# A decoder trunk in fp32: the norm between sub-layers with wide sums and a wide root, and the first chunk's products in two sums

## The chip, the core and the metric

One core of one Trainium2 chip. The metric is the time of one execution of the program on the device, in microseconds (us), as the median over runs. TensorE multiplies matrices, VectorE, ScalarE and GpSimd work elementwise, SyncE starts most DMA transfers.

## The reference

Two layers, each with three sub-layers: an FFN (half step), a token mixer with three attention branches, and a second FFN. 256 tokens, 1024 channels, float32. Between one sub-layer and the next stand two RMS norms, one on the output y of the old sub-layer and one on the new residual x:

```python
def rms_norm(x, g):
    xf = x.astype(jnp.float32)
    y = xf * lax.rsqrt(jnp.mean(xf * xf, axis=-1, keepdims=True) + EPS)
...
def swiglu(h, w_gate, w_up, w_down):
    return (jax.nn.silu(h @ w_gate) * (h @ w_up)) @ w_down

def modulate(x, g_pre, shift, scale):
    return rms_norm(x, g_pre) * (1 + scale) + shift

def residual_add(x, y, g_post, gate, res_w):
    return x + res_w * (1 + gate) * rms_norm(y, g_post)
...
        h = modulate(x, norm_pre[l, 0], mod[:, 0, 0], mod[:, 0, 1])
        x = residual_add(x, swiglu(h, ffn_w_gate[l, 0], ffn_w_up[l, 0], ffn_w_down[l, 0]), norm_post[l, 0], mod[:, 0, 2], 0.5)
        h = modulate(x, norm_pre[l, 1], mod[:, 1, 0], mod[:, 1, 1])
```

## The kernel before

Channels lie on the 128 partitions, in KC = 8 chunks; the 256 tokens lie along the free dimension. Every activation and weight is split into a high part in a reduced float32 format (fp32r) and the low rest, and each product is three matmuls, high x high, high x low and low x high (`mm3`, L170). Weights come from HBM through SyncE's queue as raw tiles of 512 KB; `wsplit` (L147) makes the high part on ScalarE (L165) and the low part on VectorE (L166). The vectors of the modulation (`modc`) come from products with `ada_w` on VectorE (L118), between other work. The framework's scheduler orders each engine's instructions by priorities and by `issue_after` pairs; each engine then runs them strictly in that order. PSUM has three banks "lin", four "att" and one "sum".

At the end of a sub-layer `out_tile` (L313) takes the eight chunks of its output: ScalarE squares them, VectorE adds up the squares of chunks 0 to 5 in `sqp`, those of chunks 6 and 7 stay apart (`sqs`); the scaled output goes to `yT`. At the start of the next, `enter` (L249) does the following.

- `mean_of` (L182) sums the squares over the channels with narrow matmuls: the squares are the stationary operand, a column of 1/n the moving one, so 128 tokens lie on the partitions of each of two columns. `rstd_from` (L194) takes the root of the 128x2 result on ScalarE (L200), its reciprocal on VectorE (L201), and spreads it over all partitions by two matmuls with a broadcast and the identity matrix (L204).
- Row k of the unnormalized new input, `acol * x`, is made for each chunk k, where `x` is the old residual plus `yT * rs`. For chunk 0, `ax` and `ay` (L258, L259) are made ahead of the root, so that one multiplication (L271) and one addition (L272) lead to the row.
- Of six weight tiles (`first`) the products of each row are summed, 18 matmuls for one k (L283), each 258 wide: two more columns carry the shift.
- In the midst of it the second norm is summed (`sqx`) with the same two functions; its root `rpre`, copied to SBUF on ScalarE (L291), scales the six results afterwards (`evac`, `evac_first`), and `finish` fills `hT`, the normalized input in high and low parts, for all further products of the sub-layer (`modulated`, L240: a VectorE, a ScalarE and a VectorE instruction for each chunk).

`enter` runs five times: for two mixers and three FFNs. The first FFN starts with `opening` (L789), which computes its norm from the input alone; after the last FFN the output norm is applied and stored (L884 to L889). Inside a mixer `sub_norm` (L441) uses the same functions for two small norms.

Of the kernel before, what the change touches and what calls it, by code (L numbers as in the profile page):

```python
# [28 lines left out]
def trunk(ctx, tc, x, c, vecs, ada_w, w_gate, w_up, w_down, w_in, w_uq, w_ukv, w_branch, w_out, rope, out):  # L29
# [22 lines left out]
    onesn = {}  # L52
    for n in (D, 256, 128):
        onesn[n] = const.tile([128, 1], F32, name=f"ones{n}")
        nc.vector.memset(onesn[n], 1.0 / n)
# [138 lines left out]
    def rstd_from(t, ahead=False):  # L194


        st = t[:, 0:2]
# [10 lines left out]
    def rstd_of(sqs, n, ahead=False):  # L208
        return rstd_from(mean_of(sqs, n, ahead), ahead)
# [15 lines left out]
    gap(res, 64, "gap0")  # L225
# [3 lines left out]
    hact = lambda i, k: hT[i][k]  # L229
    FIRST = 2176  # L230
# [18 lines left out]
    def enter(l, s, first, lent):  # L249

        acol = small.tile([128, KC], F32, name="acol")
        scale_col(l, s, acol)
        ax, ay = small.tile([128, S], F32, name="sq"), sqx
        with tc.high_priority(offset=2000):
            nc.vector.tensor_scalar(ax, xT[0], acol[:, 0:1], None, op0=OP.mult)  # L258
            nc.vector.tensor_scalar(ay, yT[:, 0, :], acol[:, 0:1], None, op0=OP.mult)  # L259
        rs, _ = rstd_of([sqp] + sqs, D, True)  # L260
        bb = modc[:, l, 3 * s, :][:, :, None].to_broadcast([128, KC, 2])
        lent = [t[:, :KC * (S + 2)].rearrange("p (k n) -> p k n", k=KC) for t in lent]
        hi, lo = [t[:, :, S:S + 2] for t in lent]
        nc.vector.tensor_copy(hi, bb)
        nc.vector.tensor_sub(lo, bb, hi.bitcast(F32))
        done = []
        for k in range(KC):
            hi, lo = [t[:, k, :] for t in lent]
            with tc.high_priority(offset=2000):
                if k == 0:  # L270
                    nc.vector.tensor_mul(ay, ay, rs)  # L271
                    head = nc.vector.tensor_add(hi[:, :S], ay, ax)  # L272
                with tc.issue_after(head.ins) if k < 2 else ExitStack():
                    nc.vector.tensor_mul(yT[:, k, :], yT[:, k, :], rs)
                nc.vector.tensor_add(xT[k], xT[k], yT[:, k, :])
                if k > 0:
                    hold[:] = [nc.scalar.activation(hi[:, :S], xT[k], AF.Copy, scale=acol[:, k:k + 1])]
                last = nc.vector.scalar_tensor_tensor(lo[:, :S], xT[k], acol[:, k:k + 1], hi[:, :S].bitcast(F32),
                                               op0=OP.mult, op1=OP.subtract)
                sum_sq(sqx, xT[k], k == 0)  # L280
            order = [(t, i, j) for i, j in ((0, 0), (1, 0), (0, 1)) for t in first]
            for (p, w, cols), i, j in (order if k < KC - 1 else sorted(order, key=lambda o: first.index(o[0]))):
                done.append(nc.tensor.matmul(p, w(i, k, cols), (hi, lo)[j], start=(k == 0 and i == j == 0),  # L283
                                             stop=(k == KC - 1 and j == 1)))
        hold.append(last)
        with tc.high_priority(offset=2000):
            with tc.issue_after(done[16 * len(first)].ins):
                t = mean_of([sqx], D, True)
            bc, _ = rstd_from(t, True)
            rp = small.tile([128, S], F32, name="rpre", bufs=1)  # L290
            nc.scalar.copy(rp, bc)  # L291

        def finish(ks=range(KC)):
            with tc.high_priority(offset=2000):
                for k in ks:
                    modulated(l, s, k, acol, bc)

        return rp, finish
# [14 lines left out]
    def out_tile(n, p, g):  # L313
        if n < KC - 1:
            if n < KC - 2:
                sum_sq(sqp, p, n == 0)
            else:
                sqs[:] = [small.tile([128, S], F32, name="pn", bufs=2) for _ in range(2)]
                nc.scalar.activation(sqs[0], p, AF.Square)
            done = nc.scalar.activation(yT[:, n, :], p, AF.Copy, scale=g[:, n:n + 1])  # L320
            if n == KC - 3:
                late[:] = [done]
        else:
            nc.scalar.activation(sqs[1], p, AF.Square)
            nc.vector.tensor_scalar(yT[:, n, :], p, g[:, n:n + 1], None, op0=OP.mult)
# [4 lines left out]
    def ffn(l, f, s, opening=None, ahead=None):  # L330
        with ExitStack() as es:
# [43 lines left out]
            if opening is None:  # L375
                todo = ([(0, n) for n in range(6)] + [(1, n) for n in range(6)] + todo[12:])
                first = [(ps(S + 2, kind="lin" if i < 3 else "att"),) + weights(*t) for i, t in enumerate(todo[:6])]
                rp, finish = enter(l, s, first, [wdp.tile([128, FIRST], F32R, name=f"wd8_{i}") for i in range(2)])
# [35 lines left out]
    def mixer(l, s):  # L414
        with ExitStack() as es:
# [25 lines left out]
            def sub_norm(src, nk, gcol, name):  # L441
# [3 lines left out]
                t = mean_of([sq], nk * 128, kind="att")  # L445
                yield
                rs, ins = rstd_from(t)
# [189 lines left out]
            first = [(ps(S + 2, kind="lin" if i < 3 else "att"), wb[i // 2], cols[i % 2]) for i in range(6)]  # L637
            gap(mp, 64, "gap2")
            rp, finish = enter(l, s, first, [mp.tile([128, FIRST], F32R, name=n) for n in ("ga", "gb")])
# [149 lines left out]
    def opening(W, evac):  # L789

        with tc.tile_pool(name="open", bufs=2) as op:
            with tc.high_priority(offset=2000):
# [9 lines left out]
                bc, _ = rstd_of([yT[:, 0, :]], D)  # L802
                rp = small.tile([128, S], F32, name="rpre", bufs=1)
                nc.scalar.copy(rp, bc)
# [173 lines left out]
```

## Time and profile before

| | us |
|---|---|
| median of 3 runs | 1303.7 (1302.9 to 1312.09) |
| profiled execution | 1309.85 |
| its span, first to last instruction | 1308.1 |
| TensorE busy (matmul) | 1267.7 (97%) |
| VectorE busy | 983.1 (75%) |
| ScalarE busy | 752.1 (57%) |

Matmuls are pipelined: the record of one is longer (0.28 us) than the distance to the next (0.11 us), so the starts of successive rows tell how fast TensorE goes. The granted clock is TensorE's clock as a share of 2.4 GHz; its two levels are 1.0 and 0.5 (1.2 GHz). A matmul in plain float32 is two records.

### The profile page before, as it was taken

To read this page: it belongs to the slowest core of one execution; us is meant where nothing else is said; L and a number is where in the kernel's file an instruction comes from. 1 tells how busy PE (TensorE), PEld (TensorE's weight loads), DVE (VectorE), ACT (ScalarE), POOL (GpSimd) and SP (SyncE) were. 2 spreads that over 40 slices of the span, in tenths; PEclk is the share of its full clock that TensorE was granted. 3 is DMA by queue.
4 is the path that set the end of the run, shared out by engine and by line. 5 is a ranking of instruction groups with operands and counts; after the bars stand their busy time and mean duration, and the time that the engine had idled before them with its cause. 6 is when DMAs were issued, how large, how long until landed. Compare 5 with 4: busy or idle time off the path is not lost. (4 is left out here: it accounts for less than half of the span.)

```text
span 1308.1 us, 26637 instructions
## 1 busy us (share of the span) xinstructions
PE 1267.7 (97%) x10752; PEld 1233.9 (94%) x10752; DVE 983.1 (75%) x1706; ACT 752.1 (57%) x1287; POOL 70.9 (5%) x140
## 2 busy tenths in 40 slices
PE   7999899999999999999999999999999999999997
PEld 6999899999899999999999999999998999999997
DVE  8987766767779789877679886585777779996553
ACT  4654454666866656445555454467567666655551
POOL 0011000000000000110000110000000000000000
PEclk9999998999999999999999999999999999999999
DMA  9997883545476666988727997626466666396550
GB/s 356 368 316 271 276 275 120 198 135 188 156 262 224 203 216 211 328 303 274 270 99 269 314 316 266 237 75 206 140 208 209 222 236 246 113 321 207 189 192 33
DMA packets 82925, 295.75 MB, mean 226 GB/s; under 512 B 9201, under 2 KB 9585, under 8 KB 82802
## 3 DMA queue, kind: packets, MB, share of 16 engines
q1 hardware_dynamic: 64370, 226.94, 50.0%
q0 software_dynamic: 18432, 67.12, 15.5%
q8 instruction: 84, 1.38, 0.4%
q14 instruction: 39, 0.32, 0.1%
HBM read 292.97 MB, written 1.05 MB: 225 GB/s over the span
## 5 line engine op out<-in xcount | busy, mean ns | idle before, releaser
L166 DVE TENSOR_TENSOR wlo<-raw,whi 128x1024 fp32r<-128x1024 f32 (+3 forms) x382 | 450.3, 1197 | 117.4 <-ACT whi L165 112.7
L171 PE MATMUL lin<-h,whi 128*128 128x256 f32 x1808 | 501.9, 279 | 4.5 <-DVE m L356 4.3
L173 PE MATMUL lin<-h,wlo 128*128 128x256 f32 x1808 | 499.3, 277 | 0.8 <-DVE wlo L166 0.8
L172 PE MATMUL lin<-h,whi 128*128 128x256 f32 x1808 | 499.3, 277 | 0.2
L165 ACT CAST whi<-raw 128x1024 fp32r<-128x1024 f32 (+3 forms) x382 | 389.4, 1034 | 172.7 <-PE lin L172 105.0
L171 PEld LDWEIGHTS lin<-h,whi 128*128 128x128 f32 x1808 | 337.8, 188 | 8.2 <-DVE m L356 5.3
L173 PEld LDWEIGHTS lin<-h,wlo 128*128 128x128 f32 x1808 | 339.7, 188 | 1.4 <-DVE wlo L166 1.4
L172 PEld LDWEIGHTS lin<-h,whi 128*128 128x128 f32 x1808 | 338.8, 188 | 1.0 <-DVE h L247 1.0
L118 DVE SCALAR_TENSOR_TENSOR ada<-ada,cb 128x1024 f32<-128x1024 f32 x128 | 154.4, 1221 | 49.5 <-DMA ada<-in_ada_w_dram 49.5
L171 PE MATMUL lin<-mid,whi 128*128 128x256 f32 x592 | 163.5, 276 | 1.1 <-DVE m L356 1.1
L172 PE MATMUL lin<-mid,whi 128*128 128x256 f32 x592 | 163.4, 276 | 0.0
L173 PE MATMUL lin<-mid,wlo 128*128 128x256 f32 x592 | 163.4, 276 | 0.0
L132 POOL DMA_DIRECT2D ada<-in_ada_w_dram x128 | 68.1, 532 | 1047.5 <-DVE ada L118 1016.3
L171 PEld LDWEIGHTS lin<-mid,whi 128*128 128x128 f32 x592 | 111.1, 188 | 1.3 <-DVE m L356 1.3
L172 PEld LDWEIGHTS lin<-mid,whi 128*128 128x128 f32 x592 | 111.1, 188 | 0.0
L173 PEld LDWEIGHTS lin<-mid,wlo 128*128 128x128 f32 x592 | 111.1, 188 | 0.0
L360 ACT CAST mid<-m 128x256 fp32r<-128x256 f32 x88 | 34.9, 409 | 115.8 <-DVE m L356 115.5
L171 PE MATMUL lin<-ybhi,whi 128*128 128x256 f32 x192 | 54.0, 281 | 2.0 <-DVE gb L514 2.0
L172 PE MATMUL lin<-yblo,whi 128*128 128x256 f32 x192 | 53.3, 278 | 0.0
L173 PE MATMUL lin<-ybhi,wlo 128*128 128x256 f32 x192 | 53.3, 278 | 0.0
L361 DVE TENSOR_TENSOR mid<-m,mid 128x256 fp32r<-128x256 f32 x88 | 36.3, 422 | 20.6 <-ACT mid L360 20.6
L171 PEld LDWEIGHTS lin<-ybhi,whi 128*128 128x128 f32 x192 | 36.1, 188 | 2.4 <-DVE gb L514 2.4
(272 smaller groups left out, 1957.4 us busy)
## 6 DMA issues: line engine op xcount, KB each, us to landing
ada<-in_ada_w_dram POOLq DMA_DIRECT2D x128, 512.0 KB, 5.7
raw<-in_mix_w_in_dram SPq DMA_DIRECT2D x100, 512.0 KB, 5.2
raw<-in_ffn_w_gate_dram SPq DMA_DIRECT2D x88, 512.0 KB, 5.8
raw<-in_ffn_w_up_dram SPq DMA_DIRECT2D x88, 512.0 KB, 6.0
raw<-in_ffn_w_down_dram SPq DMA_DIRECT2D x80, 512.0 KB, 5.1
raw<-in_mix_w_branch_dram SPq DMA_DIRECT2D x24, 512.0 KB, 6.9
oada<-in_ada_w_dram SPq DMA_DIRECT2D x16, 512.0 KB, 7.6
raw<-in_mix_w_out_dram SPq DMA_DIRECT2D x16, 512.0 KB, 5.0
```

The source lines that it names most:

```text
L118: return nc.vector.scalar_tensor_tensor(raw, raw, 1.0, cb, op0=OP.mult, op1=OP.mult, accum_out=modc[:, l, i, k:k + 1])
L132: nc.gpsimd.dma_start(raw, ada_w[al, i * D + k * 128:i * D + k * 128 + 128, :])
L165: nc.scalar.copy(hi, raw)
L166: nc.vector.tensor_sub(lo, raw, hi.bitcast(F32))
L171: nc.tensor.matmul(o, whi, ahi, start=start, stop=False)
L172: nc.tensor.matmul(o, whi, alo, start=False, stop=False)
L173: nc.tensor.matmul(o, wlo, ahi, start=False, stop=stop)
L360: nc.scalar.copy(mid[0][n], m)
L361: anchor[:] = [nc.vector.tensor_sub(mid[1][n], m, mid[0][n].bitcast(F32))]
```

## The change

- `mean_of` sums with a stationary 128x128 matrix of -1 (`negones`), the squares moving: one 128x256 float32 matmul for each tile of squares, and the sum stands on all partitions. `rstd_from` takes the root of the 128x256 result (scale -1/n) and the reciprocal 256 wide; the matmuls that spread it and the copies to SBUF go.
- `out_tile` adds the squares of chunk 6 to `sqp` too; chunk 7 alone stays apart.
- `enter` makes row 0 twice: once of the residual alone (`xrow`, with the shift's columns), once of the update alone (`yT * rs * acol`, 256 wide). Both are multiplied with the six weight tiles and summed in the same bank: 36 matmuls for chunk 0 in place of 18. The residual's first six products stand ahead of the last matmul of the sum of squares, its other twelve behind it. `xrow` lies in the last chunks of `hT`, or in the FFN's weight buffers behind a mixer. The residual's chunk 0 is updated behind chunk 1's.
- Four of the six first results lie in "att" banks and two in "lin" banks (three and three before).

```diff
-    def mean_of(sqs, n, ahead=False, kind="sum"):
-        t = ps(512, kind=kind)
-        st = t[:, 0:2]
+    def mean_of(sqs, ahead=False, kind="sum", behind=None):
+        t = ps(kind=kind)
         for i, sq in enumerate(sqs):
-            with tc.high_priority(offset=2000 if ahead and i == len(sqs) - 1 else 0):
-                for h in range(2):
-                    nc.tensor.matmul(st[:, h:h + 1], sq[:, h * 128:(h + 1) * 128], onesn[n],
-                                     start=(i == 0 and h == 0), stop=(i == len(sqs) - 1), skip_group_check=True)
+            with ExitStack() as es:
+                if behind is not None and i == len(sqs) - 1:
+                    es.enter_context(tc.issue_after(behind()))
+                es.enter_context(tc.high_priority(offset=2000 if ahead else 0))
+                nc.tensor.matmul(t, negones, sq, start=i == 0, stop=i == len(sqs) - 1, skip_group_check=True)
         return t
...
-            rs = small.tile([128, 2], F32, name="rs")
-            ins = nc.scalar.activation(rs, st, AF.Sqrt, bias=epst)
+            rs = small.tile([128, S], F32, name=name, bufs=1)
+            ins = nc.scalar.activation(rs, t, AF.Sqrt, bias=epst, scale=-1.0 / n)
             nc.vector.reciprocal(rs, rs)
-            bc = t[:, 256:512]
-            for h in range(2):
-                nc.tensor.matmul(bc[:, h * 128:(h + 1) * 128], rs[:, h:h + 1].to_broadcast([128, 128]), ident,
-                                 start=True, stop=True, skip_group_check=True)
-        return bc, ins
+        return rs, ins
...
+            nc.scalar.activation(xrow[0][:, :S], xT[0], AF.Copy, scale=acol[:, 0:1])
+            nc.vector.scalar_tensor_tensor(xrow[1][:, :S], xT[0], acol[:, 0:1], xrow[0][:, :S].bitcast(F32),
+                                           op0=OP.mult, op1=OP.subtract)
+            nc.vector.tensor_scalar(ay, yT[:, 0, :], acol[:, 0:1], None, op0=OP.mult)
...
+        def x_part():
+            products(xrow, slice(0, S + 2), 0, start=True, which=((0, 0),))
+            return done[-1].ins
+
+        rs, _ = rstd_from(mean_of([sqp] + sqs, True, behind=x_part), D, True)
+        products(xrow, slice(0, S + 2), 0, which=((1, 0), (0, 1)))
...
                 if k == 0:
-                    nc.vector.tensor_mul(ay, ay, rs)
-                    head = nc.vector.tensor_add(hi[:, :S], ay, ax)
-                with tc.issue_after(head.ins) if k < 2 else ExitStack():
+                    head = nc.vector.tensor_mul(hi, ay, rs)
+                with tc.issue_after(head.ins):
                     nc.vector.tensor_mul(yT[:, k, :], yT[:, k, :], rs)
...
+            products(row, slice(0, S + 2 if k else S), k, stop=k == KC - 1)
         hold.append(last)
         with tc.high_priority(offset=2000):
-            with tc.issue_after(done[16 * len(first)].ins):
-                t = mean_of([sqx], D, True)
-            bc, _ = rstd_from(t, True)
-            rp = small.tile([128, S], F32, name="rpre", bufs=1)
-            nc.scalar.copy(rp, bc)
+            t = mean_of([sqx], True, behind=lambda: done[19 * len(first)].ins)
+            rp, _ = rstd_from(t, D, True, "rpre")
...
         if n < KC - 1:
-            if n < KC - 2:
-                sum_sq(sqp, p, n == 0)
-            else:
-                sqs[:] = [small.tile([128, S], F32, name="pn", bufs=2) for _ in range(2)]
-                nc.scalar.activation(sqs[0], p, AF.Square)
+            sum_sq(sqp, p, n == 0)
```

How the rows of the engines move. In the names, `mid` is the FFN's inner activation, `wd_0` and `wd_1` its weights, `pn` the squares of the last chunk, `ga` and `gb` the rows of `enter` in the first mixer, `h_132` and `h_133` (in `hT`) the residual's row. TensorE before, end of the first FFN and start of the first mixer:

```order
L171 MATMUL lin<-mid_21_171,wd_0_2538 128x256
L172 MATMUL lin<-mid_21_193,wd_0_2538 128x256
L173 MATMUL lin<-mid_21_171,wd_1_2539 128x256
L190 MATMUL sum<-ones_86,sqp 128x1 x2
L190 MATMUL sum<-ones_86,pn 128x1 x4
L204 MATMUL sum<-ident,rs 128x128 x2
L283 MATMUL lin<-ga,whi 128x258 x3
L283 MATMUL att<-ga,whi 128x258 x3
L283 MATMUL lin<-ga,wlo 128x258 x3
```

TensorE of the change, the end of the same last output tile:

```order
L167 MATMUL lin<-mid_18_162,wd_0_2527 128x256
L168 MATMUL lin<-mid_18_184,wd_0_2527 128x256
L187 MATMUL sum<-sqp,negones 128x256
L169 MATMUL lin<-mid_18_162,wd_1_2528 128x256
L167 MATMUL lin<-mid_19_163,wd_0_2527 128x256
```

and some rows on, up to the first products:

```order
L167 MATMUL lin<-mid_21_165,wd_0_2527 128x256
L168 MATMUL lin<-mid_21_187,wd_0_2527 128x256
L169 MATMUL lin<-mid_21_165,wd_1_2528 128x256
L263 MATMUL lin<-h_132,whi 128x258 x2
L263 MATMUL att<-h_132,whi 128x258 x4
L187 MATMUL sum<-pn,negones 128x256
L263 MATMUL lin<-h_132,wlo 128x258 x2
L263 MATMUL att<-h_132,wlo 128x258 x4
L263 MATMUL lin<-h_133,whi 128x258 x2
L263 MATMUL att<-h_133,whi 128x258 x4
L263 MATMUL lin<-ga,whi 128x256 x2
L263 MATMUL att<-ga,whi 128x256 x4
```

The sum of `sqp` has moved into the last tile's products, the residual's products stand around the last sum, and the broadcast (L204) is gone.

VectorE before, end of the first mixer and start of the second FFN; here `wd_0` and `wd_1` hold the rows of `enter`, `wlo` is a low part of weights:

```order
L217 TENSOR_TENSOR sqp<-sqp,sq 128x256
L166 TENSOR_TENSOR wlo<-raw,whi 128x1024 x4
L325 TENSOR_SCALAR yT<-lin,gcol 128x256
L201 RECIPROCAL rs<-rs 128x2
L264 CAST wd_0_6031<-modc 128x8x2
L265 TENSOR_TENSOR wd_1_6032<-modc,wd_0_6031 128x8x2
L271 TENSOR_TENSOR sqx<-sqx,sum 128x256
L272 TENSOR_TENSOR wd_0_6031<-sqx,sq 128x256
```

VectorE of the change, the same place:

```order
L207 TENSOR_TENSOR sqp<-sqp,sq 128x256
L162 TENSOR_TENSOR wlo<-raw,whi 128x1024 x2
L207 TENSOR_TENSOR sqp<-sqp,sq 128x256
L162 TENSOR_TENSOR wlo<-raw,whi 128x1024 x2
L252 CAST wd_0_6026<-modc 128x2
L252 CAST wd_0_6024<-modc 128x7x2
L255 SCALAR_TENSOR_TENSOR wd_1_6027<-xT,acol,wd_0_6026 128x256
L253 TENSOR_TENSOR wd_1_6027<-modc,wd_0_6026 128x2
L253 TENSOR_TENSOR wd_1_6025<-modc,wd_0_6024 128x7x2
L330 TENSOR_SCALAR yT<-lin,gcol 128x256
L195 RECIPROCAL rpost<-rpost 128x256
L277 TENSOR_TENSOR wd_0_6024<-sqx,rpost 128x256
```

The addition of the seventh square now stands between the four splits of weights, and the shift's columns and the residual's low part have come ahead of L330 (L325 before) and of the reciprocal.

## Rows read from the trace of the kernel before

**Rows 1.** The page: granted TensorE clock, tenths of full speed, 40 slices of 32.7 us

```profile
PEclk9999998999999999999999999999999999999999
```

**Rows 2.** Waits: engine, line, what it waited for; us in total, times, longest

```profile
PE sum L204 <- DVE rs L201: 4.3, 7, 0.7
...
PE lin L171 <- ACT rot L708: 3.6, 2, 1.8
```

**Rows 3.** Timeline of TensorE, an FFN's end: start, length (us), [idle before, for whom]

```profile
206.53 0.50 PE L190 MATMUL sum<-ones,sqp 128*128 128x1 f32 x4
...
208.47 0.71 PE L204 MATMUL sum<-ident,rs 128*128 128x128 f32 x4 [0.55 <-DVE rs L201]
210.25 0.98 PE L283 MATMUL lin<-ga,whi 128*128 128x258 f32 x3 [1.06 <-DVE ga L272]
```

**Rows 4.** Timeline, the same end: ScalarE, then VectorE

```profile
204.69 0.39 ACT L319 ACTIVATE pn<-lin 128x256 f32<-128x256 f32 x1 [2.28 <-PE lin L173]
...
206.73 0.38 ACT L324 ACTIVATE pn<-lin 128x256 f32<-128x256 f32 x1 [1.29 <-PE lin L173]
...
209.68 0.42 DVE L272 TENSOR_TENSOR ga<-sqx,sq 128x256 fp32r<-128x256 f32 x1
```

**Rows 5.** Timeline, a mixer's end: TensorE, then VectorE

```profile
1109.28 0.50 PE L190 MATMUL sum<-ones,sqp 128*128 128x1 f32 x4
...
1113.13 0.60 PE L283 MATMUL lin<-wd,whi 128*128 128x258 f32 x3 [1.06 <-DVE wd L272]
...
1106.22 4.62 DVE L166 TENSOR_TENSOR wlo<-raw,whi 128x1024 fp32r<-128x1024 f32 x4
1110.76 0.48 DVE L325 TENSOR_SCALAR yT<-lin,gcol 128x256 f32<-128x256 f32 x1
```

**Rows 6.** Stretches behind two starts: us, busy PE, PEld, DVE, ACT, POOL, PEclk, DMA, GB/s

```profile
210.30:217.00 6.70, 6.70 (x34) 6.70 (x35) 6.70 (x20) 3.55 (x9) 0.00 (x0) 0.55 0.01 2
...
474.90:479.50 4.60, 4.60 (x26) 4.60 (x27) 4.60 (x14) 1.97 (x5) 0.00 (x0) 0.63 0.66 252
```

**Rows 7.** Stretches behind the two waits for L708

```profile
346.00:349.50 3.50, 3.50 (x19) 3.50 (x18) 3.42 (x6) 2.91 (x8) 0.00 (x0) 0.51 0.20 81
...
985.00:988.50 3.50, 2.98 (x24) 2.59 (x23) 3.42 (x6) 3.36 (x11) 0.00 (x0) 1.00 0.21 87
```

**Rows 8.** Lines L201, L551, L302: VectorE rows, ns min/median/max

```profile
L201 DVE RECIPROCAL rs<-rs x16: 153/166/166, 10.8 to 1299.0; 128x2 f32<-128x2 f32 x16
...
L551 DVE RECIPROCAL r<-sm x32: 145/160/167, 315.4 to 1054.3; 128x2 f32<-128x2 f32 x32
...
L302 DVE TENSOR_SCALAR shift<-lin x15: 148/149/152, 230.3 to 1132.5; 128x1 f32<-128x1 f32 x15
```

**Rows 9.** Timeline of TensorE: an fp32 matmul 256 wide, in two records

```profile
268.33 0.28 PE L173 MATMUL lin<-h,wlo 128*128 128x256 f32 x1
268.44 0.59 PE L589 MATMUL att<-P,negtri 128*128 128x256 f32 x2
268.88 0.38 PE L590 MATMUL att<-P,negones 128*128 128x128 f32 x2
```

**Rows 10.** Timeline of TensorE: the second norm amid the first products

```profile
1126.32 0.50 PE L190 MATMUL sum<-ones,sqx 128*128 128x1 f32 x4
1126.68 0.49 PE L283 MATMUL lin<-wd,wlo 128*128 128x258 f32 x2
...
1127.96 0.60 PE L204 MATMUL sum<-ident,rs 128*128 128x128 f32 x4
```

**Rows 11.** Timeline of VectorE: the first rows for hT

```profile
1129.01 0.87 DVE L244 SCALAR_TENSOR_TENSOR pn<-xT,acol,sum 128x256 f32<-128x256 f32 x2 [0.55 <-ACT rpre L291]
```

**Rows 12.** Timeline of VectorE: the first normalized row of the opening

```profile
12.76 0.48 DVE L824 SCALAR_TENSOR_TENSOR pn<-xT,acol,rpre 128x256 f32<-128x256 f32 x1 [0.26 <-ACT rpre L804]
```

**Rows 13.** Timeline, the end: TensorE's sums, VectorE's first output

```profile
1297.28 0.50 PE L190 MATMUL sum<-ones,sqp 128*128 128x1 f32 x4
...
1299.97 0.95 DVE L887 TENSOR_TENSOR yT<-yT,sum 128x768 f32<-128x768 f32 x1 [0.80 <-PE sum L204]
```

More of the change, by code (lines that the diff above doesn't have):

```diff
@@ L51, in trunk @@
     nc.vector.tensor_copy(identb, ident)
[L52 to L55, printed above, removed]
     epst = const.tile([128, 1], F32, name="epst")
@@ L223, in gap @@
         pool.tile([128, nbytes // 4], F32, name=name)
-    gap(res, 64, "gap0")
+    gap(res, 160, "gap0")
     hTt = [res.tile([128, KC, S], F32R, name=f"h{i}") for i in range(2)]
@@ L229, in trunk @@
     hact = lambda i, k: hT[i][k]
+    xrow_h = [t[:, KC - 2:, :].rearrange("p k n -> p (k n)")[:, :S + 2] for t in hTt]
     FIRST = 2176
@@ L247, in modulated, with enter @@
         anchor[:] = [nc.vector.scalar_tensor_tensor(lo, t, b, hi.bitcast(F32), op0=OP.add, op1=OP.subtract)]
-    def enter(l, s, first, lent):
+    def enter(l, s, first, lent, xrow):
         acol = small.tile([128, KC], F32, name="acol")
         scale_col(l, s, acol)
[L256 to L260, printed above, removed]
+        ay = sqx
@@ new lines, in enter, with products @@
+        done = []
+        def products(act, cols_of, k, start=False, stop=False, which=((0, 0), (1, 0), (0, 1))):
+            order = [(t, i, j) for i, j in which for t in first]
+            for (p, w, cols), i, j in (order if not stop else sorted(order, key=lambda o: first.index(o[0]))):
+                done.append(nc.tensor.matmul(p[:, cols_of], w(i, k, cols), act[j][:, cols_of], start=start and i == j == 0,
+                                             stop=stop and j == 1, skip_group_check=True))
@@ L267, in enter @@
+        def x_part():
[3 more added lines that the diff above has]
+        products(xrow, slice(0, S + 2), 0, which=((1, 0), (0, 1)))
         for k in range(KC):
-            hi, lo = [t[:, k, :] for t in lent]
+            row = [t[:, k, :] for t in lent]
+            hi, lo = [t[:, :S] for t in row]
             with tc.high_priority(offset=2000):
                 if k == 0:
-                    nc.vector.tensor_mul(ay, ay, rs)
-                    head = nc.vector.tensor_add(hi[:, :S], ay, ax)
-                with tc.issue_after(head.ins) if k < 2 else ExitStack():
+                    head = nc.vector.tensor_mul(hi, ay, rs)
+                with tc.issue_after(head.ins):
@@ L281, in enter @@
[L281 to L284, printed above, removed]
+                if k == 0:
+                    head = nc.vector.scalar_tensor_tensor(lo, yT[:, 0, :], acol[:, 0:1], hi.bitcast(F32),
+                                                          op0=OP.mult, op1=OP.subtract)
+                else:
+                    add = nc.vector.tensor_add(xT[k], xT[k], yT[:, k, :])
+                    if k == 1:
+                        head = add
+                    hold[:] = [nc.scalar.activation(hi, xT[k], AF.Copy, scale=acol[:, k:k + 1])]
+                    last = nc.vector.scalar_tensor_tensor(lo, xT[k], acol[:, k:k + 1], hi.bitcast(F32),
+                                                          op0=OP.mult, op1=OP.subtract)
+                    if k == 1:
+                        with tc.issue_after(head.ins):
+                            nc.vector.tensor_add(xT[0], xT[0], yT[:, 0, :])
+                        sum_sq(sqx, xT[0], True)
+                    sum_sq(sqx, xT[k], False)
@@ L323, in out_tile @@
         else:
-            nc.scalar.activation(sqs[1], p, AF.Square)
+            sqs[:] = [small.tile([128, S], F32, name="pn", bufs=2)]
+            nc.scalar.activation(sqs[0], p, AF.Square)
             nc.vector.tensor_scalar(yT[:, n, :], p, g[:, n:n + 1], None, op0=OP.mult)
@@ L376, in ffn @@
                 todo = ([(0, n) for n in range(6)] + [(1, n) for n in range(6)] + todo[12:])
-                first = [(ps(S + 2, kind="lin" if i < 3 else "att"),) + weights(*t) for i, t in enumerate(todo[:6])]
-                rp, finish = enter(l, s, first, [wdp.tile([128, FIRST], F32R, name=f"wd8_{i}") for i in range(2)])
+                first = [(ps(S + 2, kind="lin" if i < 2 else "att"),) + weights(*t) for i, t in enumerate(todo[:6])]
+                rp, finish = enter(l, s, first, [wdp.tile([128, FIRST], F32R, name=f"wd8_{i}") for i in range(2)],
+                                   [wdp.tile([128, S + 2], F32R, name=f"wd16_{i}") for i in range(2)] if s == 2 else xrow_h)
                 evac(*todo[0], first[0][0], rp)
@@ L444, in sub_norm @@
                     sum_sq(sq, src[:, k, :], k == 0)
-                t = mean_of([sq], nk * 128, kind="att")
+                t = mean_of([sq], kind="att")
                 yield
-                rs, ins = rstd_from(t)
+                rs, ins = rstd_from(t, nk * 128, name="rpost" if nk > 1 else "rpre")
                 hi = mp.tile([128, nk, S], F32R, name=name + "hi")
@@ L636, in mixer @@
             wb = [win(1536 + 256 * i, 256) for i in range(3)]
-            first = [(ps(S + 2, kind="lin" if i < 3 else "att"), wb[i // 2], cols[i % 2]) for i in range(6)]
+            first = [(ps(S + 2, kind="lin" if i < 2 else "att"), wb[i // 2], cols[i % 2]) for i in range(6)]
             gap(mp, 64, "gap2")
-            rp, finish = enter(l, s, first, [mp.tile([128, FIRST], F32R, name=n) for n in ("ga", "gb")])
+            rp, finish = enter(l, s, first, [mp.tile([128, FIRST], F32R, name=n) for n in ("ga", "gb")], xrow_h)
             qkb = mp.tile([128, 8, S], F32, name="km")
@@ L801, in opening @@
                 nc.vector.tensor_add(yT[:, 0, :], yT[:, 0, :], yT[:, 1, :])
-                bc, _ = rstd_of([yT[:, 0, :]], D)
-                rp = small.tile([128, S], F32, name="rpre", bufs=1)
-                nc.scalar.copy(rp, bc)
+                rp, _ = rstd_of([yT[:, 0, :]], D, name="rpre")
             acol = small.tile([128, KC], F32, name="acol")
```

22 lines of the change are left out of this document (8 added, 14 removed).

## The prediction

> **What bounds the kernel now.** I read the page first, then the waits of TensorE, then the timeline of each engine around one change of sub-layer, then the stretches with their granted clock.
>
> TensorE is busy nearly all the time. What it loses is in few places: the row of the granted clock has its only dips there [rows 1], and the waits of TensorE name them: seven times it waits for the root of the output norm (L201) [rows 2]; five of these stand at the start of a sub-layer. Such starts are the entry of two mixers and of three FFNs (the first FFN has an opening of its own). One of them, at an FFN's end: the last product is issued just before T = 206.53, and the first product of the mixer starts at 210.25, 3.72 us later [rows 3]. In between stands a chain: Square on ScalarE [rows 4], twelve narrow sums, root, reciprocal, broadcast matmuls, a multiplication and an addition on VectorE. At a mixer's end it is 3.85 us, from 1109.28 to 1113.13, and VectorE comes to it with four splits of weights still queued [rows 5].
>
> Behind each such gap the clock is at 1.2 GHz for a while: 0.55 of full speed over 6.70 us once, 0.63 over 4.60 us at the four others (one stands for them) [rows 6]. Lost: 0.45 x 6.70 + 4 x 0.37 x 4.60 = 9.8 us. So the five starts cost 5 x 3.8 us of gap and 9.8 us of clock, some 29 us, 2% of the span.
>
> **The chain of the output norm.** Step by step from T at an FFN's end. The running sum sqp now takes row 6 as well, and its matmul stands in TensorE's row 10 products ahead of the last. Its turn comes at T - 10 x 0.113 = 205.40 (0.11 us a product, L173 to L589 [rows 9]); Square of row 6 ended at 204.69 + 0.39 = 205.08 [rows 4], the addition on VectorE (0.42 us, as any 256-wide one with two operands [rows 4]) at 205.53, so TensorE waits 0.13 us. A 128x256 fp32 matmul takes 0.44 us of the row (L589 to L590) [rows 9]. The last product is thus over at T + 0.6. Square of row 7 then runs to T + 1.2; meanwhile TensorE does the first six x products, 258 wide, so 0.12 each, to T + 1.3, then the last sum, to T + 1.75. The root, 256 wide, takes about what Square takes, 0.42 with its start: T + 2.25. Then the reciprocal, then a multiplication 0.45, and 0.15 until the product starts (L272 ends at 210.10, the product starts at 210.25) [rows 3, 4].
>
> **What the trace does not show: a reciprocal 256 wide.** It shows it 2 wide, with medians of 166 and 160 ns at two lines and 167 ns as the longest; a one-column operation takes 149 ns [rows 8]. If it streams like other VectorE operations, 256 elements take 0.42 us. If what the two elements take above 149 ns is their price, it is 5.5 to 9 ns each, 1.6 to 2.4 us in all. I take 2.0 us, since the rows of the operation itself are the nearest ones, and keep 0.42 and 2.4 as ends.
> The Trainium skill (VectorE: DVE Perf Modes, "First, the fixed hardware budget") says that Reciprocal is an iterative divide with a repeat count of 8. Read as 8 cycles of its 0.96 GHz for each element, an estimate by that page is 2.13 + 0.15 = 2.3 us, and the sum below would be +7 in place of +5 us; no row here shows it.
>
> With 2.0 us the products of the update start at T + 2.25 + 2.0 + 0.45 + 0.15 = T + 4.85, against T + 3.72 before: **+1.1 us at three starts**. The other twelve x products end at T + 1.75 + 12 x 0.12 = T + 3.2 and then TensorE waits 1.7 us. The 18 x products are work added (2.15 us), hidden in the chain either way. The 18 products of the update take the place of the old first row's 18.
> At a mixer's end VectorE sets the time. Its reciprocal stood behind L325, which started at 1110.76 and held the queue some 0.4 us, to 1111.15 [rows 5]. Now an addition and the low x part, 0.4 us each, and two more small copies, 0.2 each, come before it and one multiplication of 0.3 goes: 0.9 us (estimates from the 256-wide rows). So the reciprocal starts at 1112.05, the update at 1112.05 + 2.0 + 0.6 = 1114.65, against 1113.13 [rows 5]: **+1.5 us at two starts**. TensorE also stands in the row for sqp, whose addition is queued behind two of the four splits, 1.15 us each; that lies inside this chain. All five: 3 x 1.1 + 2 x 1.5 = +6.3 us.
>
> **The clock.** A wait of 1.7 us after six and then twelve products is shorter than the gap before. The trace holds two waits of 1.8 us at full speed, both for L708 [rows 2]: behind one, at 345, the clock fell to 0.51, behind the other, at 984, it stayed [rows 7]. So I count half of 9.8 us regained, -4.9 (ends: 0 and -9.8).
>
> **The second norm** (of the new residual, in the midst of the first products): four narrow sums (1126.32 to 1126.68) and four broadcast records (0.60 with their ends, some 0.4 of the row) go; one 0.44 us matmul comes [rows 10]: -0.3 us each, -1.4 in all. Its reciprocal lies off TensorE's path but in VectorE's queue ahead of the rows that fill hT, which the next products read. A ScalarE copy and a broadcast round trip go, 1.8 us of reciprocal comes; I take 0.5 us each, +2.5 (ends 0 and +9.0).
>
> **The rest.** Opening: VectorE waits only 0.26 us for the root's copy [rows 12]; the reciprocal now stands behind both products with ada_w: +1.2 (ends +0.1 and +2). End: the sums started at 1297.28 and the first output at 1299.97, 2.69 us [rows 13]; now 0.6 + 0.44 + 0.46 for sums and root, 2.0 and two issues, 3.56: +0.9. Four inner norms of the mixer, under products of other pieces: +0.5. The high and low x parts are made before the last product ends, under it.
>
> **Sum:** 6.3 - 4.9 - 1.4 + 2.5 + 1.2 + 0.9 + 0.5 = +5.1 us. The profiled execution of before took 1309.85 us (span 1308.1 and 1.75 around it), so 1315.0 for one like it; the median of the runs is 1303.7, 6.15 lower, and on that scale the forecast is 1308.8, +0.4%. Its own range, by the clock's ends and the reciprocal's, is 1301 to 1316.
>
> **Rivals.**
> *The wide reciprocal streams* (0.42 us). For it: the other 256-wide VectorE rows shown take 0.42 and 0.48 us [rows 4, 5]; against it: the 11 to 18 ns above. Then the update starts at T + 3.27 at an FFN's end (-0.45 x 3), at 1113.07 at a mixer's (-0.1 for both), TensorE's x products end at T + 3.2, so it hardly waits and the clock stays: -9.8. Second norm -1.4, end -0.7, opening +0.1: -13.2, **1290.5**.
> *VectorE's queue behind the first products decides.* The first row for hT came at 1129.01 [rows 11]; if the 1.8 us of the second reciprocal reach TensorE whole at all five starts (+9.0 in place of +2.5), and the clock falls at four of five (-2.0 in place of -4.9): 5.1 + 6.5 + 2.9 = +14.5, **1318.2**, slower. It decides once VectorE, between the end of the first products and the last row of hT, has no idle time left; for it speaks that VectorE is busy all through the stretch behind a start [rows 6], against it the 0.55 us in which it idles before that first row [rows 11].
> *A price in between*, 1 us: the start comes 0.5 us later at two places and 0.1 at three, the clock stays: about -6, **1298**.
>
> **How the numbers follow.** Forecast 0.42, streaming 0.38, VectorE's queue 0.15, in between 0.05. One per cent, about what a measurement of this kernel can tell from no change, is 1290.7 and 1316.7. Faster by more: half of the streaming case and a little, 0.22. Slower by more: most of the queue's case and the upper end of the forecast's, 0.16. Within: 0.62. The range takes in the middle of the streaming case with some 2 us below it, and the queue's: 1288 to 1318.
>
> **What would show it.** The row of the reciprocal 256 wide on the changed line: 1.6 us or more makes the forecast or the queue's case, 0.45 or less the streaming one. The start of the first product with ga or wd after the last product of the sub-layer: T + 4.9 or T + 3.3. The row of the granted clock: dips at two or three of five, or at none. The stretch of 7 us behind the first products: fewer matmuls in it than before means that the queue's case is at work. I would be wrong altogether if TensorE stood for the sums' matmul in the middle of the last products for over a microsecond, or if the x products waited for their weights' low parts.

## The result, and the profile after

The changed kernel took 1328.99 us (median of 4 runs, 1327.54 to 1331.92), the kernel before 1307.89 us (4 runs, 1302.9 to 1322.0): 1.014 of it, 95% interval 1.0095 to 1.0186. The forecast was 1308.8 us with a range to 1318: it is slower, and outside the range. The forecast stands on the 1303.7 us of the first three runs; in the rounds of the experiments the kernel before had medians of 1310.7 to 1314.7 us. So part of the distance in microseconds is the base. As a ratio, the top of the range (1.011 of its base) lies inside the interval, and the forecast itself (1.004) below it. The profiled executions took 1328.8 and 1309.85 us, their spans are 1327.1 and 1308.1 us: 19.0 us to be explained.

The page after, granted clock:

```profile
PEclk9999999999999999999999999999999999999999
```

The dip of [rows 1] is gone. That row could show only the longest dip, at the first start; the four shorter ones of [rows 6] do not bring a slice of 32.7 us below 9 tenths. So the stretches behind two starts have to tell (columns as in [rows 6]; 144 products each):

```profile
212.50:230.00 17.50, 17.48 (x144) 17.45 (x145) 17.04 (x38) 10.04 (x20) 0.00 (x0) 1.00 0.15 40
...
477.50:495.00 17.50, 17.50 (x145) 17.37 (x145) 17.03 (x40) 10.21 (x21) 0.00 (x0) 1.00 0.19 63
```

Clock 1.00 where it was 0.55 and 0.63. In the same rows VectorE is busy 17.0 of 17.5 us; that will matter. The reciprocal 256 wide, by its line:

```profile
L195 DVE RECIPROCAL rpre<-rpre x8: 1694/1746/1748, 11.9 to 1141.0; 128x256 f32<-128x256 f32 x8
L195 DVE RECIPROCAL rpost<-rpost x8: 1745/1752/1753, 210.2 to 1317.2; 128x256 f32<-128x256 f32 x8
```

1.75 us, near the 2.0 us that were taken. A start at an FFN's end, timeline of TensorE, ScalarE and VectorE, which answers to [rows 3] and [rows 4]:

```profile
206.60 0.70 PE L187 MATMUL sum<-sqp,negones 128*128 128x256 f32 x2
206.95 0.47 PE L169 MATMUL lin<-mid,wd 128*128 128x256 f32 x1
...
208.28 0.40 PE L263 MATMUL lin<-h,whi 128*128 128x258 f32 x2
...
209.00 0.61 PE L187 MATMUL sum<-pn,negones 128*128 128x256 f32 x2
...
212.52 0.47 PE L263 MATMUL lin<-ga,whi 128*128 128x256 f32 x2 [1.45 <-DVE ga L277]
...
209.66 0.48 ACT L194 ACTIVATE rpost<-sum,epst 128x256 f32<-128x256 f32 x1 [0.79 <-PE sum L187]
...
210.16 1.75 DVE L195 RECIPROCAL rpost<-rpost 128x256 f32<-128x256 f32 x1 [0.78 <-ACT rpost L194]
```

With T = 208.28, the first residual product, the last sum stands at T + 0.72, the root at T + 1.38, the update's first product at T + 4.24. TensorE idles 1.45 us and keeps its clock of 1.00. The waits of TensorE now (what it waited for; total, times, longest):

```profile
PE lin L167 <- ACT h L237: 3.0, 5, 0.7
PE lin L263 <- DVE ga L277: 2.9, 2, 1.5
PE lin L168 <- DVE h L238: 2.7, 3, 0.9
```

The first and the third were not among the waits of before: products wait for hT. What the waits do not show is the larger part. Stretches of 20 us amid the second matrix of one FFN (products with mid as the moving tile); first before, then after:

```profile
610.00:630.00 20.00, 20.00 (x179) 20.00 (x178) 14.13 (x20) 10.53 (x16) 1.59 (x3) 1.00 0.78 265
```

```profile
610.00:630.00 20.00, 20.00 (x171) 20.00 (x170) 12.11 (x17) 7.39 (x12) 1.58 (x3) 1.00 0.65 209
```

TensorE is busy for all 20 us at a clock of 1.00 in both, and does 179 products in the one and 171 in the other (each count includes the two or three under way at the left edge). Products start every 0.1133 us before and every 0.1190 us after, on 1774 products of this kind. Busy share and clock tell nothing of it: only the count does.

**Where the 19.0 us are.** Each start is read from the timeline in two parts: from the last product of the sub-layer to the first product that reads hT, and from there to the 240th such product.

| part | before | after | difference |
|---|---|---|---|
| opening: first product with h | 14.13 | 15.03 | +0.9 |
| five starts, last product to first with hT | 119.2 | 113.8 | -5.4 |
| five starts, from there to the 240th | 176.2 | 186.6 | +10.4 |
| products with mid: 1774 x (0.1190 - 0.1133) | | | +10.1 |
| products with yb: 576 x (0.1186 - 0.1148); with h and weights in the mixer's tiles: 126 x (0.1198 - 0.1134) | | | +3.0 |
| end: last product with mid to the end | 10.96 | 11.94 | +1.0 |
| rest | | | -1.0 |

### The profile page after: what moved, and what is told of

Its sections match the earlier page's. It is cut to its first block, busy times and chain, and to the rows that moved or that the text cites. A ratio compares the mean times of both kernels' runs of the same rounds, so it can differ in the third digit from the quotient of the medians.

```text
span 1327.1 us, 26607 instructions
## 1 busy us (share of the span) xinstructions
PE 1277.8 (96%) x10710; PEld 1237.9 (93%) x10710; DVE 1012.6 (76%) x1714; ACT 755.1 (57%) x1286; POOL 70.6 (5%) x140
## 3 DMA queue, kind: packets, MB, share of 16 engines
q8 instruction: 84, 1.38, 0.4%
## 4 chain that ended last, share of the span: by engine, by line
PE 58%; DVE 4%; ACT 3%; issue 1%; DMA 0%; SPq 0%
PE lin L167 17%; PE lin L169 17%; PE lin L168 17%; PE att L263 3%; PE lin L263 2%; DVE wlo L162 1%; DVE h L238 1%; DVE rpost L195 1%; PE sum L531 1%; PE sum L187 1%; DVE pn L235 1%; ACT whi L161 1%; DMA raw<-in_mix_w_out_dram 0%; PE att L566 0%; PE att L541 0%
## 5 line engine op out<-in xcount | busy, mean ns | idle before, releaser
L167 PE MATMUL lin<-mid,whi 128*128 128x256 f32 x592 | 166.6, 281 | 1.2 <-DVE m L361 1.2
L169 PE MATMUL lin<-mid,wlo 128*128 128x256 f32 x592 | 167.1, 282 | 0.0
L168 PE MATMUL lin<-mid,whi 128*128 128x256 f32 x592 | 166.9, 282 | 0.0
L207 DVE TENSOR_TENSOR sqp<-sqp,sq 128x256 f32<-128x256 f32 x36 | 15.2, 422 | 42.0 <-ACT sq L206 42.0
```

The source lines that it names most:

```text
L167: nc.tensor.matmul(o, whi, ahi, start=start, stop=False)
L168: nc.tensor.matmul(o, whi, alo, start=False, stop=False)
L169: nc.tensor.matmul(o, wlo, ahi, start=False, stop=stop)
L207: anchor[:] = [nc.vector.tensor_add(acc, acc, sq)]
```

## Experiments

Two theories stood against each other and against chance. *Placement:* the products became slower because their tiles lie elsewhere. Two rs tiles, 32 bytes each in the pool, left the pool of small tiles and rpost, 1024 bytes, came into it: all pools behind it lie 960 bytes higher, which is 64 bytes lower modulo 1024; the widened gap0 keeps h, yT and the weight tiles where they were. *VectorE's queue:* the two long reciprocals delay hT. In the expectations quoted below, "behind a mixer's end" means all three entries of an FFN, and "behind an FFN's end" the two entries of a mixer.

**e1, the changed kernel with its tiles moved back.**

```diff
     gap(res, 64, "gap1")
+    small.tile([128, 16], F32, name="pad", bufs=1)
```

> The changed kernel with one unused tile of 64 bytes per partition in the pool of small tiles, so that all pools behind it (mid, weights of the down products, the mixer's tiles) lie where they lay in the kernel before, modulo 1024 bytes; nothing else. Theory 'placement': the products that stream mid and the mixer's yb tiles start every 0.113 us again instead of 0.119, which is 3 x 592 + 1152 products by 0.006 us = 10 + 7 us at most; the time falls from 1329 to about 1316 (1312 to 1319). Rival 'not placement' (the closer spacing was lost to the fuller stream of products or to another reader of memory): spacing stays 0.119 and the time 1329.

Measured: 1319.62 us, 1.0067 of before (1.0039 to 1.0094), just above the expected 1312 to 1319. The count is back:

```profile
610.00:630.00 20.00, 20.00 (x179) 20.00 (x179) 14.25 (x20) 10.22 (x16) 1.59 (x3) 1.00 0.72 243
...
740.00:760.00 20.00, 20.00 (x173) 20.00 (x172) 15.73 (x23) 9.58 (x15) 2.12 (x4) 1.00 0.85 284
```

So some nine of the 21 us were placement. That the gain is no larger may be due to stretches like the second row: products with h, at its old place, that were slow in this execution. Which stretches are slow so differs from trace to trace; more of them below.

**e2, the kernel before with those pools moved.** The same line in the kernel before, with 960 bytes (240 elements).

> The kernel before with one unused tile of 960 bytes in the pool of small tiles: the pools behind it lie at the addresses of the changed kernel, and nothing else changes. Theory 'placement': spacing of the products with mid and yb rises from 0.113 to 0.119 us and the time from 1308 to about 1321 (1317 to 1325). Rival 'not placement': no change.

Measured: 1323.82 us, 1.0091 (1.0057 to 1.0124), with not one instruction of the kernel changed:

```profile
615.00:635.00 20.00, 20.00 (x169) 20.00 (x169) 12.24 (x17) 9.00 (x12) 1.58 (x3) 1.00 0.69 232
```

Placement alone costs some 13 us (7 to 16 by the interval).

**e8, another place.** As e1, with 32 bytes (8 elements).

> The changed kernel with an unused tile of 32 bytes in the pool of small tiles instead of e1's 64, so that mid begins at 0 modulo 128 bytes (before: 32, changed kernel: 96, while the weights begin at 96 and h at 32). Theory 'slow where the moving tile and the weights begin at the same place modulo 128 bytes': spacing of the products with mid 0.113 us as in e1. Rival 'only the old place is fast': 0.119 us.

Measured: 1331.37 us (one run), products with mid and the weight tiles every 0.1180 us, x173 in 20 us. So "slow where both begin at the same place" is not the whole of it: at a distance of 32 they are slow as well. The two traces hold a finer test. Some products with mid take their weights from wd tiles, which moved together with mid. In the changed kernel, at one clock (5 us each, first weights whi and wlo, then wd):

```profile
650.00:655.00 5.00, 5.00 (x45) 5.00 (x44) 3.31 (x4) 4.61 (x7) 0.00 (x0) 1.00 0.63 244
659.00:664.00 5.00, 5.00 (x47) 5.00 (x46) 0.50 (x1) 0.42 (x2) 0.00 (x0) 1.00 0.96 357
```

The same mid is slow with weights that stayed and not with weights that moved along. VectorE and ScalarE have little to do in the second row, but that is not the reason: over all products of mid with whi and wlo in this trace, the spacing is 0.1189 us where neither of the two works (395 products) and 0.1190 us where both do (558). The distance between the two tiles decides, then, which the next run tests from the other side.

**e9, the kernel before, weights moved against h.**

```diff
     sqx = res.tile([128, S], F32, name="sqx")
+    gap(res, 64, "gap5")
```

> The kernel before with an unused tile of 64 bytes behind sqx, so that the weight tiles and all that lies behind them move up by 64 bytes together, while h stays. Modulo 128 bytes h then begins where the weights begin (both 32; before 32 and 96), as mid and the weights did in the changed kernel (both 96); mid and the mixer's yb tiles keep their distance of 64 from the weights. Theory 'relation': products whose moving tile begins where the weight tile begins, modulo 128 bytes, start every 0.118 to 0.119 us; so the products with h (some 5500, of which the profile of before has about 0.84 at 0.113) become slow, those with mid and yb stay at 0.113: 5500 x 0.84 x 0.0055 = 25 us more, 1310 + 25 = 1335 (1325 to 1340). Rival 'mid's own address': mid has moved, so its products go to 0.119 (+10 us) and those with h stay: 1320. Rival 'neither': 1310.

Measured: 1332.05 us, 1.0169 (1.0131 to 1.0207). Stretches of products with h, then with mid twice:

```profile
560.00:580.00 20.00, 20.00 (x171) 20.00 (x170) 16.35 (x22) 9.99 (x15) 2.11 (x4) 1.00 0.84 291
624.00:644.00 20.00, 20.00 (x179) 20.00 (x178) 13.83 (x21) 10.80 (x14) 1.58 (x3) 1.00 0.81 285
...
810.00:830.00 20.00, 20.00 (x172) 20.00 (x172) 13.34 (x20) 9.94 (x16) 1.59 (x3) 1.00 0.77 251
```

Now h, which did not move, is slow nearly throughout, and mid is so in some stretches only. Mean time from start to start, by the distance of the two tiles' first bytes modulo 128:

| moving tile, weights | kernel | distance | us |
|---|---|---|---|
| mid, whi and wlo | before / e1 | 64 | 0.1133 / 0.1144 |
| mid, whi and wlo | after / e2 | 0 | 0.1190 / 0.1193 |
| mid, wd | after / e2 | 64 | 0.1138 / 0.1135 |
| mid, whi and wlo | e8 | 32 | 0.1180 |
| mid, wd | e8 | 64 | 0.1146 |
| mid, whi and wlo | e9 | 64 | 0.1156 |
| h, whi and wlo | before / after | 64 | 0.1143 / 0.1145 |
| h, whi and wlo | e1 / e2 / e8 | 64 | 0.1155 / 0.1154 / 0.1154 |
| h, whi and wlo | e9 | 0 | 0.1189 |
| h, ga and km | before / after | 64 / 0 | 0.1134 / 0.1198 |

These means are mixtures. Taken over 90 products in a row, the spacing at each distance has two values, nearly always one of them for a whole stretch: 0.1133 or 0.1178 us at 64, 0.1173 or 0.1187 at 32, 0.1187 or 0.1200 at 0. The distance shifts both values: from 64 to 0 it costs 0.0054 or 0.0022 us a product. Which of the two values a stretch has (the longer one in e1 at 740 us and in e9 at 810 us) is not explained by distance and stays open.

**e3, the second norm by the old route** (in the changed kernel; tiles at their old places).

```diff
-            t = mean_of([sqx], True, behind=lambda: done[19 * len(first)].ins)
-            rp, _ = rstd_from(t, D, True, "rpre")
+            t = mean_n([sqx], D, True, behind=lambda: done[19 * len(first)].ins)
+            bc, _ = root_n(t, True)
+            rp = small.tile([128, S], F32, name="rpre", bufs=1)
+            nc.scalar.copy(rp, bc)
...
-                    modulated(l, s, k, acol, rp)
+                    modulated(l, s, k, acol, bc)
```

Here mean_n and root_n are mean_of and rstd_from of the kernel before.

> The changed kernel with the second norm (over the new residual) by the old route: the sum as two columns, a root and a reciprocal of 2 elements, two broadcast products, and a copy on ScalarE. Its small tiles also put the pools behind them back to their old places modulo 1024. Theory 'VectorE's queue at the second norm': against e1 the gaps of TensorE ahead of the products with h behind the first products, 4.2 us in each FFN now, go back to about 1.1: 3 x 3 and some 1.5 for the mixers, so 1316 - 10 = 1306 (1303 to 1310). Rival 'the gaps come from the order in which VectorE now makes the updates, and not from the long reciprocal': the gaps stay and the time is e1's.

Measured: 1315.6 us, 1.0043 (1.0009 to 1.0076), 4 us less than e1 where 10 were expected, and above the expected 1303 to 1310; by the time alone the two are not told apart, for their intervals overlap. The five starts show the effect: first hT product to the 240th takes 177.5 us in all, against 189.2 in e1 and 176.2 before. Of these 11.7 us, 11.4 are gaps between products and not their spacing. The longer wait for hT goes with the second norm's wide root, and the rival is out.

**e7, that reciprocal twice** (e1 with one more, its result unused).

```diff
             ins = nc.scalar.activation(rs, t, AF.Sqrt, bias=epst, scale=-1.0 / n)
+            if twice:
+                nc.vector.reciprocal(small.tile([128, S], F32, name="rpost", bufs=1), rs)
             nc.vector.reciprocal(rs, rs)
```

> Kernel e1 (changed kernel, tiles at the old places) with one more reciprocal of 256 elements on VectorE right ahead of the second norm's own, its result unused. Theory 'VectorE's queue bounds the stretch from the first root to the last chunk of hT': the 240th product behind a mixer's end goes from T + 54.7 to T + 56.3 and behind an FFN's end from T + 68.5 to T + 70: five times 1.6 us, so 1319.6 + 8 = 1328. Rival 'the waits come from the order, and VectorE has slack': less than 0.4 us each, 1320 to 1321.5.

Measured: 1339.14 us, 1.0224 (1.0143 to 1.0306): 19.5 over e1, more than twice the 8 expected. VectorE's timeline says why:

```profile
491.62 1.74 DVE L196 RECIPROCAL rpost<-rpre 128x256 f32<-128x256 f32 x1
493.28 1.16 DVE L162 TENSOR_TENSOR wlo<-raw,whi 128x1024 fp32r<-128x1024 f32 x1
494.36 1.74 DVE L197 RECIPROCAL rpre<-rpre 128x256 f32<-128x256 f32 x1
496.01 1.16 DVE L162 TENSOR_TENSOR wlo<-raw,whi 128x1024 fp32r<-128x1024 f32 x1
```

Between the two reciprocals the order puts one more split of a weight tile, 1.16 us. So the step costs 2.7 us; the first product with hT comes 3.0 us later at each start (128.3 us in all against 113.3), and behind the idle 3.3 us the granted clock falls (0.50 from 230.4 to 236.0 us, where it was 1.00 in the changed kernel). So the effect is there, larger than forecast; part of it is the clock's.

**e5, the wide roots alone, on the kernel before.** Both norms at a start, one sum for chunk 0.

```diff
-        rs, _ = rstd_of([sqp] + sqs, D, True)
+        rs = wide_of([sqp] + sqs, D, True)
...
-                t = mean_of([sqx], D, True)
-            bc, _ = rstd_from(t, True)
-            rp = small.tile([128, S], F32, name="rpre", bufs=1)
-            nc.scalar.copy(rp, bc)
+                rp = wide_of([sqx], D, True, "rpre")
```

Here wide_of is the sum by negones, the root and the reciprocal of the changed kernel.

> The kernel before with one part of the change alone: at the start of a sub-layer both norms take their sum on all partitions and a root and reciprocal 256 wide; chunk 0 still goes as one sum. Its tiles behind the small ones lie at the old places modulo 1024 bytes. Theory 'VectorE's queue': the first reciprocal delays the first products by 3.8 - 2.97 = 0.85 us (to T + 4.7) and, with the second one, hT by about 3 us, so that the 240th product with h behind a mixer's end comes at T + 55 instead of T + 52, and behind an FFN's end at T + 71 instead of 69.4; over five starts about 12 us: 1323 (1317 to 1328). Rival 'TensorE's row of first products hides the roots': only the 0.85 us of five starts, less the two broadcast products saved: 1313.

Measured: 1323.65 us, 1.0104 (1.0009 to 1.0198). The time is in the expected range; but against the kernel before in the same rounds (1314.69) it is 9 us more, not 12, and the interval is too wide to exclude the rival. The trace decides: entries of an FFN reach the 240th product at T + 54.5 to 56.4 (52 before). VectorE at one start, where the first product comes 5.3 us behind the sub-layer's last instead of 4.0 (+1.3, where 0.85 was expected):

```profile
469.72 1.75 DVE L216 RECIPROCAL rpost<-rpost 128x256 f32<-128x256 f32 x1
471.50 0.42 DVE L282 TENSOR_TENSOR sqx<-sqx,rpost 128x256 f32<-128x256 f32 x1
```

**e4 and e11, the two sums without the wide roots.** e4 is e3 with the first norm narrow too, its broadcast behind the residual's products; e11 is e4 with the inner norms, the opening and the end narrow as well.

```diff
-        rs, _ = rstd_from(mean_of([sqp] + sqs, True, behind=x_part), D, True)
+        t = mean_n([sqp] + sqs, D, True, behind=x_part)
         products(xrow, slice(0, S + 2), 0, which=((1, 0), (0, 1)))
+        rs, _ = root_n(t, True, done[-1].ins)
```

> As e3, with the first norm's root narrow too (two columns, broadcast by two products behind the residual's products); the two sums stay. Theory 'the 1.75 us reciprocal stands on the path at the start': update products start about 0.7 to 0.9 us earlier at each of five starts (from T + 4.24 to about T + 3.4), so e3 less 4: 1302 (1299 to 1306). Rival 'residual products and the row behind them cover it': e3's time.

> The two sums of chunk 0 at all five starts as in the changed kernel, and every norm by the old narrow route (sum as two columns, root and reciprocal of 2 elements, two broadcast products), the inner norms, the opening and the end too; all tiles at the old places. From e4's trace: the five stretches from a sub-layer's last product to the 240th product with h sum to 294.6 us against 295.4 before, and the opening and the end lose what the wide root cost there (0.9 + 1.0 us). Theory 'the start's gain is given back at hT, VectorE being no earlier': within 0.3% of the kernel before, 1307 to 1315 against 1311. Rival 'the regained clock pays': 1.0 to 2.0 us at each start, 1301 to 1306.

Measured: e4 1315.79 us, 1.0048 (1.0011 to 1.0085); e11 1318.12 us, 1.0033 (1.0005 to 1.0061). e4 missed the expected 1299 to 1306 and came out at e3's time, as its rival had it; e11, 5.7 us over the kernel before in its own rounds, is slower than both of its forecasts had it. The clock of e11's profile is 0.998 as in the changed kernel, and it brings nothing. In e4 the update starts only 0.5 us earlier than with the wide root, at T + 3.77, since the broadcast now stands in the chain (timeline of TensorE; the first residual product is at T = 206.85):

```profile
209.50 0.61 PE L224 MATMUL sum<-ident,rs 128*128 128x128 f32 x4
210.62 0.51 PE L293 MATMUL lin<-ga,whi 128*128 128x256 f32 x2 [0.51 <-DVE ga L308]
```

The five starts in e4: 112.1 us to the first hT product (7 less than before), then 182.4 to the 240th (6 more). What TensorE gains it waits out at hT, because VectorE makes hT no earlier: at a mixer's end its last low part is done 33.0 us behind the sub-layer's last product, against 31.4 before and 31.9 in e3. The order puts one more split of a weight tile ahead of it (six, against five in both of these).

**e6 and e10, the new start at the two mixers alone.** The kernel before, with enter of the changed kernel (wide first root, narrow second) called by the mixer only, out_tile as changed only in the FFN ahead of it.

> The kernel before with the new start (two sums for chunk 0, wide first root; second root narrow) at the two mixers alone; the three FFN starts, the inner norms, the opening and the end as before. Theory 'the new start pays where VectorE has little to do behind it': the 240th product with h behind an FFN's end at about T + 67.1 instead of 70.6 and 69.4, the rest unchanged: 5.8 less, 1305 against 1310.7. Rival 'what is gained at the start is lost until the sub-layer's end anyway': no change, 1311.

> Kernel e6 again, over more rounds: the new start at the two mixers alone. By e6 it stands at 0.996 of the kernel before; theory 'VectorE has room behind an FFN's end' expects 0.996 again (0.993 to 0.999), the rival 'no difference' 1.000.

Measured: 1308.97 us, 0.9961 (0.9924 to 0.9997), then 1312.22 us, 1.0017 (0.999 to 1.0044): e6 as expected, e10 outside its 0.993 to 0.999 and with the rival. The trace has the gain where it was expected, 68.0 us at both entries of a mixer against 70.4 and 69.2 before; as a time it is not larger than what the second measurement can tell from nothing. No version is shown to beat the kernel before.

## Why the prediction was wrong, point by point

**The step that failed is one the prediction never took:** that everything away from the starts, the opening, the end and the inner norms stays as it is. It weighed instructions and waits; the placement of tiles was not in it, though the diff shows it (gap0 from 64 to 160, rs out, rpost in). So the sum has nothing for it. It cost 13.1 us by the trace's products, 9 us by e1 and 13 us by e2. The forecast was +5.1; e1, the change without it, is 1.0067 of before, +9 us: beside the placement the forecast lies at the lower end of what was measured (5 to 12 us).

**The starts:** forecast +6.3. Measured at an FFN's end: T + 4.24 (forecast 4.85, before 3.72), so +0.5 three times; at a mixer's end +1.1 twice (forecast +1.5): +3.8. The reciprocal was right to 0.25 us; the sums were too dear, since the last sum runs at T + 0.72 and not behind T + 1.3. At a mixer's end the number came near by luck. VectorE's queue was to set the time there, with both parts of the residual's row made before the last product ends. In the trace ScalarE starts the high part only when the last product (472.13 to 472.41) has ended, the residual's products wait 0.60 us for it, and VectorE, its queue done, waits 0.96 us for the root:

```profile
472.44 0.51 ACT L254 ACTIVATE wd<-xT,acol 128x256 fp32r<-128x256 f32 x1 [1.29 <-PE lin L169]
...
474.98 1.75 DVE L195 RECIPROCAL rpost<-rpost 128x256 f32<-128x256 f32 x1 [0.96 <-ACT rpost L194]
```

The measured 1.75 us for 256 elements, less 0.15 us for one column [rows 8], is 6.25 ns an element. The Trainium skill (VectorE: DVE Perf Modes, "First, the fixed hardware budget") gives the divide a repeat count of 8, and read as 8 cycles an element this had given 2.3 us; 6.25 ns are 6 cycles of that page's 0.96 GHz. The measurement decides.

**The clock:** forecast -4.9, half of the loss. Measured: the 144 products that followed a gap took 19.6 us four times and 20.8 once, the same 144 now 17.7 each: -10.6, the whole loss of 9.8 with what the second norm's sum gave in the same row. (The five starts show -5.4 and not 3.8 - 10.6, since the first product with hT now waits 0.3 us behind that row.) The idle time ahead of the update's products, 1.35 us at a mixer's end and 1.45 us at an FFN's, left the clock at 1.00.

**The second norm and hT:** forecast -1.4 in the row, which is counted above, and +2.5. Measured from the first product with hT to the 240th: +10.4. The rival "VectorE's queue behind the first products decides" had this right (+9.0 at most was its price) and had the clock wrong. The sign that was named for it came out: in the 7 us behind the first products TensorE does 46 matmuls at each of the five starts, where it did 52 to 55. From the sub-layer's last product to the last row of hT VectorE is idle for 0.6 to 1.4 us, where it was 2.4 to 5.5 before; the second reciprocal and what the order puts beside it push all rows of hT back. Its rows at a mixer's end, before and after (T = 470.87 and 472.13 for the sub-layer's last product):

```profile
490.74 0.87 DVE L244 SCALAR_TENSOR_TENSOR pn<-xT,acol,sum 128x256 f32<-128x256 f32 x2 [0.56 <-ACT rpre L291]
...
501.42 0.87 DVE L247 SCALAR_TENSOR_TENSOR h<-pn,modc,h 128x256 fp32r<-128x256 f32 x2
```

```profile
491.09 1.75 DVE L195 RECIPROCAL rpre<-rpre 128x256 f32<-128x256 f32 x1
492.75 1.16 DVE L162 TENSOR_TENSOR wlo<-raw,whi 128x1024 fp32r<-128x1024 f32 x1
...
494.16 0.48 DVE L235 SCALAR_TENSOR_TENSOR pn<-xT,acol,rpre 128x256 f32<-128x256 f32 x1
...
505.86 0.48 DVE L238 SCALAR_TENSOR_TENSOR h<-pn,modc,h 128x256 fp32r<-128x256 f32 x1
```

The first row for hT went from T + 19.9 to T + 22.0, the last low part from T + 31.4 to T + 34.2: 2.8 us, about the reciprocal (1.75) and one more split (1.15) in that stretch, six where there were five. VectorE's idle 0.55 us ahead of the first row [rows 11], which had spoken against the rival, was no cover for both.

**Opening and end:** forecast +1.2 and +0.9, measured +0.9 and +1.0. The four inner norms could not be told apart from the rest.

So two terms were far off in opposite directions: the clock with the row's -1.4 by 4 us (forecast -6.3, measured -10.6), hT by 8 (forecast +2.5, measured +10.4). That the starts as a whole came out near (forecast +2.5, measured +5.0) is luck. The size of the miss is the placement.

## What to carry to other kernels

When a change adds or drops a tile, compare the tiles' addresses before its instructions: count the products in a stretch where TensorE is busy throughout, in both kernels, and the slower spacing shows at once. An engine's idle time won back at the head of a stretch is worth only what the next engine in the chain can follow: before it is booked, see whether the engine that makes the next operand has any idle time left. A long operation put into a full queue can cost more than its own length, since the order may let other work in beside it (2.7 us for 1.74 in e7).

## What the runs showed of the hardware that was not expected

Products of 128x256 start every 0.113 us or every 0.117 to 0.120 us at the same granted clock, TensorE being busy without a gap in both cases. The distance between the first bytes of the moving tile and of the weight tile, modulo 128, sets it to a large part: at 0 and 32 products are slow, at 64 a large part is fast, on tiles moved from either side (e1, e2, e8, e9). At each distance there are two values, one for a whole stretch: 0.1133 and 0.1178 us at 64, 0.1187 and 0.1200 at 0. At 64 the share of products with h and the weight tiles at the longer one is 15% to 47% over the traces, with one trace for each kernel (two for that of e6 and e10); whether a change to the kernel alters this share is not shown. What decides between the two, and why the distance matters, was not found.
